# The final RMSNorm of a decoder trunk: other roots, other order, and a wider filling tile

## The chip, the cores and the metric

The kernel runs on one core of one Trainium2 chip. The metric is the device time of one execution in microseconds (us), as the median of several runs. Engines are named as in the profile: PE is TensorE (matmuls), DVE is VectorE, ACT is ScalarE, POOL is GpSimd, SP is SyncE, which here only issues DMAs. Before the change the median of three runs is 1943.36 us (1942.74 to 1943.45).

## The reference

One layer of a hybrid decoder works on 1024 tokens of width 1024 in float32. Three token mixers feed a gated merge, then comes an MLP, and a last RMSNorm over each token's row gives the output. Only the end matters here:

```python
    h = h + jnp.einsum('bsd,de->bse', merged, w_out[l])
    hn = rms_norm(h, norm_mlp_g[l])
    up = jax.nn.relu(jnp.einsum('bsd,df->bsf', hn, w_mlp_up[l]))
    h = h + jnp.einsum('bsf,fd->bsd', up * up, w_mlp_down[l])
    return rms_norm(h, final_norm_g)

def rms_norm(x, g):
    y = x * lax.rsqrt(jnp.mean(x * x, axis=-1, keepdims=True) + EPS)
    return y * g
```

So each output row is h times the gain g, times one root per row: 1/sqrt(mean of the row's squares + EPS).

## The kernel before, in words

Tokens lie in eight row blocks of 128 (0 to 7, one token per partition), and each row block of h is a tile `H[c]` of 128 by 1024, with a left half (`hsl(0)`) and a right half (`hsl(1)`) of 512 columns.

The second MLP product h + up·w_dn runs over the hidden width in four sets (`j`), each a scheme of seven bursts (`i`, 0 to 6) in place of eight plain block products. A burst is four products (`p`, 0 to 3). A product is twelve 128x512 matmuls (`seventh`, line 487: operands are split in a high and a low part, and three of the four part products are taken), and DVE then adds its result from PSUM into one half of one row block (line 1625). In the last set the order of the bursts sets which halves become final:

- burst 3: left halves of row blocks 0 to 3; burst 4: their right halves. After burst 4 these rows are finished.
- burst 5: right halves of row blocks 4 to 7; burst 6: their left halves. After burst 6 the product is at its end.

A generator (`advance(dn)`) prepares later bursts' operands between the products: ACT copies to the high part (line 132) and DVE subtracts for the low part (line 133, 128x1024), called a split below. The last three splits fall in burst 4, behind the adds of its first three products. Everything stands in a manual schedule: each engine runs its instructions in the order in which the code issues them.

The final RMSNorm, before:

- In bursts 3 to 6, behind each add, ACT squares the finished half and sums it into a column of its own (line 1843; the sum is written by a second instruction, ACTIVATION_READ_ACCUMULATOR).
- In burst 5, behind the add for row block p+4, DVE multiplies that half by the gain (line 1846), then forms the root of row block p in ten one-column instructions (`row_scale`, line 1808; `rsqrt_col`, lines 107 to 112: a bit-trick start and three Newton steps), and multiplies the whole row block p by root and gain (line 1848, 128x1024). SP stores its two halves (line 1804).
- In burst 6, POOL (for the first three) or DVE (for the last) multiplies the left half by the gain (line 1853); one product later DVE forms the root in the same ten instructions, ACT multiplies both halves by it (lines 1820 and 1816), and SP stores them. The last row block follows behind the loop; there DVE does the left half (line 1823).

A pool of small columns (`small`) holds the sums and roots; it begins with an unused tile of `SPACER` columns (line 84). Pools allocated behind it (`act`, `act1`, `act2`, `half` and others, which hold operands) lie above it, so their addresses hang on its size.

## Time and profile before

| what | value |
|---|---|
| median of three runs | 1943.36 us |
| the profiled execution's own time | 1942.18 us |
| its span, first to last instruction | 1940.5 us |
| outside the span | 1.68 us |
| PE, DVE, ACT, POOL busy | 98%, 73%, 52%, 13% |
| PE's last matmul ends | 1923.85 us after the span's start |
| from there to the end of the span | 16.65 us |

The profile has a page (busy times, chain of waits, groups of instructions) and views of the trace: the timeline lists instructions with start, duration, engine, line, operation, what is written and read, and in brackets the engine's idle time ahead of it with what ended it. The windows view gives busy times of each engine in stretches of the span. `a`, `b`, `wt`, `rt` are 128x1024 tiles of four pools, `aux` a PSUM tile, `fs` and `roots` columns. A start is in us from the start of the span.

### The profile page before, as it was taken

Reading aid. Unit: us, or ns where it says so; the run is one execution under the profiler, and the core shown is the slowest. Engines: PE = TensorE matmul, PEld = TensorE weight load, DVE = VectorE, ACT = ScalarE, POOL = GpSimd, SP = SyncE. Lnnn points to the kernel's source line nnn. Section 1 sums busy time; section 2 is a strip of 40 time slices with the busy share of each in tenths; the row PEclk is TensorE's granted clock in tenths of the full one; section 3 lists DMA queues with packets and bytes.
Section 4 is the critical chain, followed back from the end, with each engine's and each line's share of the span. In section 5 each row is a group of like instructions: output and inputs, shape, how many; then the busy total and the mean of one; then the engine's idle time right before and its main releaser. Section 6 shows DMA issues by size and latency. Waiting matters only on the chain.

```text
span 1940.5 us, 23747 instructions
## 1 busy us (share of the span) xinstructions
PE 1895.9 (98%) x8928; PEld 1581.8 (82%) x8928; DVE 1415.9 (73%) x2047; ACT 1005.3 (52%) x1463; POOL 259.0 (13%) x355
## 2 busy tenths in 40 slices
PE   8999999999999999999999999999999999999996
PEld 7998888888887787878778888887788887888885
DVE  6585868787758767677777888367666567788787
ACT  6435859676534545454554544265555555343253
POOL 4112112122342010000010110000121110000000
PEclk9999999999999999999999999999999999999998
DMA  5346575575755343434398987431553458454532
GB/s 164 77 137 141 115 157 123 122 159 136 164 137 157 110 143 110 150 106 135 113 293 276 256 233 192 152 111 49 184 201 131 168 186 282 166 163 126 178 120 87
DMA packets 211015, 301.25 MB, mean 155 GB/s; under 512 B 13028, under 2 KB 125876, under 8 KB 210900
## 3 DMA queue, kind: packets, MB, share of 16 engines
q1 hardware_dynamic: 167348, 158.54, 26.6%
q0 software_dynamic: 34544, 119.69, 23.1%
q10 hardware_dynamic: 9008, 21.51, 3.1%
q8 instruction: 70, 1.15, 0.2%
q14 instruction: 45, 0.37, 0.1%
HBM read 195.75 MB, written 74.58 MB: 139 GB/s over the span
## 4 chain that ended last, share of the span: by engine, by line
PE 81%; DVE 9%; issue 4%; ACT 3%; DMA 3%; POOL 1%; ACTq 0%; SPq 0%; POOLq 0%; DVEq 0%
PE aux L487 40%; PE ps L564 16%; PE gps L487 11%; PE aux L1387 4%; PE aux L257 4%; PE aux L800 1%; DMA raw<-in_w_in_dram 1%; PE aux L736 1%; PE aux L732 1%; DVE wt L133 1%; ACT wt L132 1%; PE aux L712 1%; PE aux L1647 1%; DVE a L133 1%; PE aux L847 0%
## 5 line engine op out<-in xcount | busy, mean ns | idle before, releaser
L564 PE MATMUL ps<-xn,wh 128*128 128x512 f32 x1088 | 295.0, 392 | 0.0
L487 PE MATMUL aux<-b,b 128*128 128x512 f32 x1152 | 264.3, 389 | 0.5 <-DVE b L133 0.5
L487 PEld LDWEIGHTS aux<-b,b 128*128 128x128 f32 x1152 | 216.0, 188 | 46.5 <-DVE b L133 1.3
L564 PEld LDWEIGHTS ps<-xn,wh 128*128 128x128 f32 x1088 | 202.9, 188 | 42.2 <-issue 0.5
L487 PE MATMUL aux<-a,b 128*128 128x512 f32 x960 | 219.4, 389 | 0.0
L487 PEld LDWEIGHTS aux<-a,b 128*128 128x128 f32 x960 | 180.2, 188 | 37.4
L564 PE MATMUL ps<-xn,wl 128*128 128x512 f32 x544 | 168.2, 389 | 0.0
L487 PE MATMUL gps<-xn,wt 128*128 128x512 f32 x684 | 158.7, 389 | 2.1 <-DVE a L238 2.1
L487 PE MATMUL aux<-b,wt 128*128 128x512 f32 x672 | 156.9, 389 | 0.0
L487 PEld LDWEIGHTS gps<-xn,wt 128*128 128x128 f32 x684 | 128.3, 188 | 29.0 <-issue 2.5
L487 PEld LDWEIGHTS aux<-b,wt 128*128 128x128 f32 x672 | 126.2, 188 | 26.2
L132 ACT ACTIVATE b<-wt 128x1024 fp32r<-128x1024 f32 x88 | 90.7, 1053 | 85.6 <-DMA wt<-u_d 63.1
L133 DVE TENSOR_TENSOR wt<-a,wt 128x1024 fp32r<-128x1024 f32 x66 | 80.8, 1225 | 65.1 <-ACT wt L132 65.0
L564 PEld LDWEIGHTS ps<-xn,wl 128*128 128x128 f32 x544 | 102.1, 188 | 21.5
L133 DVE TENSOR_TENSOR b<-wt,b 128x1024 fp32r<-128x1024 f32 x88 | 107.1, 1218 | 15.7 <-ACT b L132 15.7
L1625 DVE TENSOR_TENSOR a<-aux,a 128x512 f32<-128x512 f32 x112 | 77.0, 688 | 50.4 <-PE aux L487 50.4
L133 DVE TENSOR_TENSOR a<-a,a 128x1024 fp32r<-128x1024 f32 (+1 forms) x68 | 66.5, 985 | 41.8 <-ACT a L132 41.7
L132 ACT ACTIVATE a<-a 128x1024 fp32r<-128x1024 f32 (+1 forms) x68 | 55.7, 834 | 53.0 <-DVE a L1577 45.6
L133 DVE TENSOR_TENSOR wt<-rt,wt 128x1024 fp32r<-128x1024 f32 x35 | 42.8, 1224 | 52.7 <-ACT wt L132 52.5
L487 PE MATMUL aux<-a,wt 128*128 128x512 f32 x336 | 78.7, 390 | 1.2 <-ACT a L1500 1.2
L132 ACT ACTIVATE wt<-a 128x1024 fp32r<-128x1024 f32 x66 | 69.6, 1055 | 12.5 <-DVE a L515 12.1
L487 PEld LDWEIGHTS aux<-a,wt 128*128 128x128 f32 x336 | 62.9, 188 | 15.0 <-ACT a L1500 2.0
(348 smaller groups left out, 3505.6 us busy)
## 6 DMA issues: line engine op xcount, KB each, us to landing
wt<-u_d SPq DMA_DIRECT2D x54, 512.0 KB
u_d<-a POOLq DMA_DIRECT2D x48, 512.0 KB, 4.9
raw<-in_w_in_dram SPq DMA_DIRECT2D x34, 512.0 KB
wl<-raw POOLq DMA_DIRECT2D x34, 512.0 KB, 5.2
g_d<-a POOLq DMA_DIRECT2D x24, 512.0 KB, 3.6
a<-g_d ACTq DMA_DIRECT2D x24, 512.0 KB
rt<-in_w_in_dram SPq DMA_DIRECT2D x19, 512.0 KB
a<-in_w_in_dram SPq DMA_DIRECT2D x19, 512.0 KB
```

Of the source, the lines that this page charges most:

```text
L132: actv(dst_hi, src, AF.Copy)
L133: (eng or nc.vector).tensor_tensor(out=dst_lo, in0=src, in1=dst_hi.bitcast(F32), op=ALU.subtract)
L257: mm(ps[:, :nt], X.tok(a, k, c), wk[k][w], start=(k == 0 and i == 0), stop=(k == KD - 1 and i == 2))
L487: mm(ps, lhs[l][kk], rhs[r][kk], start=(new and n == 0), stop=(n == 11), skip_group_check=not new)
L564: mm(ps[:, hsl(h)], w[wi][:, k, :], a.rhs(ai, k, h), start=(n == 0), stop=(n == 3 * KD - 1))
L712: mm(st[:, cc * 256:cc * 256 + 256], Bt[:, 2 * q + cc, :], xw[q][:, cc].rearrange("p h d -> p (h d)"), start=True, stop=True)
L732: mm(yo[:, tok(i)], pv[c // 2][:, c % 2, j * P:(j + 1) * P], Cf[:, tok(c)], start=True, stop=True)
L736: mm(yi[64 * h:64 * h + 64, tok(i)], xdt[c // 2][:, c % 2, 2 * j + h, :], E[c // 2][:, c % 2, 2 * j + h, :], start=True, stop=True)
L800: mm(ps, w[wi][:, q * P:(q + 1) * P], S["xs"][half][ai], start=(n == 0), stop=(n == 2))
L1387: mm(ps, M.tok(a, k, c), wo[nb][k][w], start=(k == 0 and a + w == 0), stop=(k == KD - 1 and a == 1))
L1625: tt(out=h, in0=ps, in1=h, op=ALU.add)
L1647: mm(ps, w[1 + l][:, k, :], f[r][k % 4], start=(n == 0), stop=(n == 3 * KD - 1))
```

## The change

The change rewrites the final RMSNorm and leaves the products alone.

- Row blocks 0 to 3: each half is multiplied by the gain (`weigh`) already in burst 4, behind its add. The roots of all four are formed once, in burst 5 behind the first add: DVE means, ACT `Sqrt` of four columns, and DVE a reciprocal with one Newton step (`roots_first`, `refine_first`). ACT then multiplies each whole row block by its root (`rows_first`), and SP stores it in one DMA of 128x1024 in place of two.
- Row blocks 4 to 7: `weigh` on DVE for every half; POOL has no part any more. In burst 6 the right half's sum becomes a column `known`; ACT takes `Sqrt` of the scaled left sum plus `known`, and five one-column DVE instructions refine it (`refine_last`). One product later DVE multiplies the left half and ACT the right one (`out_half`). The very last store is issued by ACT's queue, all others by SP's.
- `SPACER` goes from 32 to 40 columns. With it the tiles of the pool `small` end at 52432 bytes (before: 52676), and the pools above it begin 256 bytes lower than before (`act2`, which holds the tiles `a` of this stage, at 52448 in place of 52704). The pools of the tiles `b`, `wt` and `rt` stay where they were.

```diff
-SPACER = 32
+SPACER = 40
...
+        def square_sum(c, nb):
+            actv(act()[:, :HF], H[c][:, hsl(nb)], AF.Square, accum_out=squares[c // half][nb][:, c % half:c % half + 1])
+        def weigh(c, nb):
+            if c not in scaled:
+                scaled[c] = act()
+            tt(out=scaled[c][:, hsl(nb)], in0=H[c][:, hsl(nb)], in1=fg[:, hsl(nb)], op=ALU.mult)
+        def out_half(c, nb, eng, queue):
+            o, rs = scaled[c][:, hsl(nb)], root[:, c % half:c % half + 1]
+            if eng is nc.vector:
+                ts(out=o, in0=o, scalar1=rs, scalar2=None, op0=ALU.mult)
+            else:
+                actv(o, o, AF.Identity, scale=rs)
+            queue.dma_start(out=out[c * P:(c + 1) * P, hsl(nb)], in_=o)
+        def rows_first(p):
+            o = scaled[p]
+            actv(o, o, AF.Identity, scale=root[:, p:p + 1])
+            nc.sync.dma_start(out=out[p * P:(p + 1) * P, :], in_=o)
+        def roots_first():
+            tt(out=mean, in0=squares[0][0], in1=squares[0][1], op=ALU.add)
+            ts(out=mean, in0=mean, scalar1=1.0 / D, scalar2=EPS, op0=ALU.mult, op1=ALU.add)
+            actv(root, mean, AF.Sqrt)
+        def refine_first():
+            nc.vector.reciprocal(out=root, in_=root)
+            tt(out=step_, in0=root, in1=root, op=ALU.mult)
+            tt(out=step_, in0=step_, in1=mean, op=ALU.mult)
+            ts(out=step_, in0=step_, scalar1=-0.5, scalar2=1.5, op0=ALU.mult, op1=ALU.add)
+            tt(out=root, in0=root, in1=step_, op=ALU.mult)
+        def root_last(p):
+            actv(root[:, q], squares[1][0][:, q], AF.Sqrt, scale=1.0 / D, bias=known[:, q])
+        def refine_last(p):
+            stt(out=mean[:, q], in0=squares[1][0][:, q], scalar=1.0 / D, in1=known[:, q], op0=ALU.mult, op1=ALU.add)
+            ts(out=mean[:, q], in0=mean[:, q], scalar1=-0.5, scalar2=None, op0=ALU.mult)
+            nc.vector.reciprocal(out=root[:, q], in_=root[:, q])
+            stt(out=step_[:, q], in0=root[:, q], scalar=mean[:, q], in1=root[:, q], op0=ALU.mult, op1=ALU.mult)
+            stt(out=root[:, q], in0=step_[:, q], scalar=1.5, in1=root[:, q], op0=ALU.add, op1=ALU.mult)
...
-                if i == 5:
-                    scaled[c] = act()
-                    tt(out=scaled[c][:, hsl(1)], in0=h, in1=fg[:, hsl(1)], op=ALU.mult)
-                    rs, o = row_scale(p), act()
-                    stt(out=o, in0=H[p], scalar=rs, in1=fg, op0=ALU.mult, op1=ALU.mult)
-                    for b in range(2):
-                        out_row(p, b, o[:, hsl(b)])
+                square_sum(c, nb)
+                if i == 4:
+                    weigh(c, 0)
+                    weigh(c, 1)
+                elif i == 5:
+                    if p == 0:
+                        roots_first()
+                    weigh(c, 1)
+                    if p == 0:
+                        refine_first()
+                    rows_first(p)
                 elif i == 6:
-                    eng = nc.gpsimd if p < 3 else nc.vector
-                    eng.tensor_tensor(out=scaled[c][:, hsl(0)], in0=h, in1=fg[:, hsl(0)], op=ALU.mult)
-                    if waiting is not None:
-                        last_rows(waiting, row_scale(waiting), by_scalar)
-                    waiting = c
-        last_rows(waiting, row_scale(waiting), by_vector)
+                    if p == 0:
+                        ts(out=known, in0=squares[1][1], scalar1=1.0 / D, scalar2=EPS, op0=ALU.mult, op1=ALU.add)
+                    root_last(p)
+                    weigh(c, 0)
+                    if p:
+                        out_half(c - 1, 0, nc.vector, nc.sync)
+                        out_half(c - 1, 1, nc.scalar, nc.sync)
+                    refine_last(p)
+        out_half(NCH - 1, 0, nc.vector, nc.sync)
+        out_half(NCH - 1, 1, nc.scalar, nc.scalar)
```

How the instructions stand on the engines. The first place is DVE in burst 5, the product of row block 5. Before, from the gain on (`a_15074`, behind the add of the same half) to the next add's predecessor, with the root of row block 1 between:

```order
L1846 TENSOR_TENSOR a_15074<-a_12959,a_14841 128x512
L1808 TENSOR_TENSOR fs_2290_14894<-fs_2290_14894,fs_2312_14984 128x1
L107 TENSOR_SCALAR rsq_r_15078<-fs_2290_14894 128x1
L108 TENSOR_SCALAR rsq_v_15077<-rsq_r_15078 128x1
L109 TENSOR_SCALAR rsq_r_15078<-rsq_r_15078 128x1
L111 SCALAR_TENSOR_TENSOR rsq_q_15079<-rsq_r_15078,rsq_v_15077 128x1
L112 SCALAR_TENSOR_TENSOR rsq_r_15078<-rsq_q_15079,rsq_r_15078 128x1
L111 SCALAR_TENSOR_TENSOR rsq_q_15079<-rsq_r_15078,rsq_v_15077 128x1
L112 SCALAR_TENSOR_TENSOR rsq_r_15078<-rsq_q_15079,rsq_r_15078 128x1
L111 SCALAR_TENSOR_TENSOR rsq_q_15079<-rsq_r_15078,rsq_v_15077 128x1
L112 SCALAR_TENSOR_TENSOR roots_13004<-rsq_q_15079,rsq_r_15078 128x1
L1848 SCALAR_TENSOR_TENSOR a_15089<-a_12998,roots_13004,a_14841 128x1024
```

With the change, DVE in burst 5 from the first add (row block 4) to the add of row block 6:

```order
L1625 TENSOR_TENSOR a_12957<-aux_2283_14850,a_12957 128x512
L1827 TENSOR_TENSOR fm_13008<-fs_1963_13004,fs_1964_13005 128x4
L1828 TENSOR_SCALAR fm_13008<-fm_13008 128x4
L1811 TENSOR_TENSOR a_15052<-a_12957,a_14848 128x512
L1832 RECIPROCAL fr_13009<-fr_13009 128x4
L1833 TENSOR_TENSOR fs_13010<-fr_13009 128x4
L1834 TENSOR_TENSOR fs_13010<-fs_13010,fm_13008 128x4
L1835 TENSOR_SCALAR fs_13010<-fs_13010 128x4
L1836 TENSOR_TENSOR fr_13009<-fr_13009,fs_13010 128x4
L1625 TENSOR_TENSOR a_12959<-aux_2289_14874,a_12959 128x512
L1811 TENSOR_TENSOR a_15076<-a_12959,a_14848 128x512
L1625 TENSOR_TENSOR a_12961<-aux_2297_14902,a_12961 128x512
```

A product had the add and twelve further DVE instructions; now the first has the add and eight, the other three the add and one.

The second place is DVE in burst 6, between the adds of row blocks 6 and 7. Before:

```order
L1625 TENSOR_TENSOR a_12961<-aux_2292_14897,a_12961 128x512
L1808 TENSOR_TENSOR fs_2350_15193<-fs_2350_15193,fs_2327_15071 128x1
L107 TENSOR_SCALAR rsq_r_15233<-fs_2350_15193 128x1
L108 TENSOR_SCALAR rsq_v_15232<-rsq_r_15233 128x1
L109 TENSOR_SCALAR rsq_r_15233<-rsq_r_15233 128x1
```

(six more of lines 111 and 112 follow, then the add of row block 7). With the change:

```order
L1625 TENSOR_TENSOR a_12961<-aux_2297_14902,a_12961 128x512
L1811 TENSOR_TENSOR a_15095<-a_12961,a_14848 128x512
L1816 TENSOR_SCALAR a_15076<-a_15076,fr_13009 128x512
L1844 SCALAR_TENSOR_TENSOR fm_13008<-fs_1965_13006,fk_13011 128x1
L1845 TENSOR_SCALAR fm_13008<-fm_13008 128x1
L1846 RECIPROCAL fr_13009<-fr_13009 128x1
L1847 SCALAR_TENSOR_TENSOR fs_13010<-fr_13009,fm_13008 128x1
L1848 SCALAR_TENSOR_TENSOR fr_13009<-fs_13010,fr_13009 128x1
L1625 TENSOR_TENSOR a_12963<-aux_2303_14926,a_12963 128x512
```

Ten one-column instructions became five, but two 128x512 ones came to DVE from POOL and ACT.

The third place is ACT at the first add of burst 5 (the sum of row block 4) and behind it, with the change; the table load, the `Sqrt` and the 128x1024 scaling had no counterpart on ACT there before:

```order
L1806 ACTIVATE a_15047,fs_1966_13007<-a_12957 128x512
L1829 ACT_TABLE_LOAD
L1829 ACTIVATE fr_13009<-fm_13008 128x4
L1823 ACTIVATE a_14969<-a_14969,fr_13009 128x1024
L1806 ACTIVATE a_15074,fs_1966_13007<-a_12959 128x512
```

With the change this is the only table load behind that of line 926: in burst 6 `Square`, `Sqrt` and `Identity` follow each other without one. PE's order is the same in both kernels.

More of the change, by code (lines that the diff above doesn't have):

```diff
@@ L1799, in trunk_kernel @@
                 prev.last_sum()
-        sums, scaled = {}, {}
-        roots = sm(NCH, "roots")
-        def out_row(c, nb, o):
-            nc.sync.dma_start(out=out[c * P:(c + 1) * P, hsl(nb)], in_=o)
-        def row_scale(c):
-            rs = roots[:, c:c + 1]
-            tt(out=sums[c, 0], in0=sums[c, 0], in1=sums[c, 1], op=ALU.add)
-            rsqrt_col(rs, sums[c, 0], 1.0 / D, EPS)
-            return rs
-        def last_rows(c, rs, left):
-            o = scaled[c]
-            left(o[:, hsl(0)], rs)
-            out_row(c, 0, o[:, hsl(0)])
-            actv(o[:, hsl(1)], o[:, hsl(1)], AF.Identity, scale=rs)
-            out_row(c, 1, o[:, hsl(1)])
@@ L1819, in by_scalar @@
-        def by_scalar(o, rs):
-            actv(o, o, AF.Identity, scale=rs)
-        def by_vector(o, rs):
-            ts(out=o, in0=o, scalar1=rs, scalar2=None, op0=ALU.mult)
-        waiting = None
+        half = NCH // 2
+        squares = [[sm(half, f"fs{th}{nb}") for nb in range(2)] for th in range(2)]
+        mean, root, step_, known = (sm(half, f"f{i}") for i in "mrsk")
+        scaled = {}
+        def square_sum(c, nb):
+            actv(act()[:, :HF], H[c][:, hsl(nb)], AF.Square, accum_out=squares[c // half][nb][:, c % half:c % half + 1])
@@ L1831, in trunk_kernel @@
                 nc.scalar.dma_start(out=fg, in_=final_norm_g.partition_broadcast(P))
-            for p in range(NCH // 2):
+            for p in range(half):
                 if n + p == 0:
```

5 lines of the change are left out of this document (2 added, 3 removed).

## The prediction

> **What bounds the kernel now.** I read the page first: PE sets the pace nearly everywhere, so a change behind PE's last matmul counts in full, and one beside it only if PE waits.
>
> ```profile
> span 1940.5 us, 23747 instructions
> PE 1895.9 (98%) x8928; PEld 1581.8 (82%) x8928; DVE 1415.9 (73%) x2047; ACT 1005.3 (52%) x1463; POOL 259.0 (13%) x355
> PE 81%; DVE 9%; issue 4%; ACT 3%; DMA 3%; POOL 1%; ACTq 0%; SPq 0%; POOLq 0%; DVEq 0%
> ```
>
> Next the windows view of the end, cut where DVE begins each product of burst 5 (columns: us, then PE, PEld, DVE, ACT, POOL busy, granted clock, DMA share, GB/s), and PE's last row of the timeline:
>
> ```profile
> 1902.13:1904.85 2.72, 2.72 (x13) 2.25 (x12) 0.69 (x1) 0.72 (x2) 0.00 (x0) 1.00 0.00 0
> 1909.49:1914.12 4.63, 4.63 (x22) 3.85 (x21) 4.25 (x14) 0.72 (x2) 0.00 (x0) 1.00 0.31 115
> 1923.85:1940.50 16.65, 0.00 (x1) 0.00 (x0) 11.36 (x46) 7.33 (x15) 3.76 (x3) 0.62 0.42 157
> 1912.81 11.04 PE L487 MATMUL aux<-b,b 128*128 128x512 f32 x48
> ```
>
> PE delivers a product every 2.72 us and ends at 1912.81 + 11.04 = 1923.85. DVE needs 4.63 us for each product of burst 5, so it falls 1.9 us behind each time, and 16.65 us pass after PE has ended. The timeline says what fills them:
>
> ```profile
> 1902.13 0.69 DVE L1625 TENSOR_TENSOR a<-aux,a 128x512 f32<-128x512 f32 x1 [0.90 <-PE aux L487]
> 1904.85 0.69 DVE L1625 TENSOR_TENSOR a<-aux,a 128x512 f32<-128x512 f32 x1 [2.03 <-PE aux L487]
> 1905.58 0.69 DVE L1846 TENSOR_TENSOR a<-a,a 128x512 f32<-128x512 f32 x1
> 1906.19 0.15 DVE L1808 TENSOR_TENSOR fs<-fs,fs 128x1 f32<-128x1 f32 x1
> 1924.20 2.49 POOL L1853 TENSOR_TENSOR a<-a,a 128x512 f32<-128x512 f32 x2 [296.31 <-DVE a L1625]
> 1926.08 0.63 DVE L111 SCALAR_TENSOR_TENSOR rsq_q<-rsq_r,rsq_v 128x1 f32<-128x1 f32 x1
> 1930.83 0.69 DVE L1625 TENSOR_TENSOR a<-aux,a 128x512 f32<-128x512 f32 x1
> 1934.32 0.72 ACT L1820 ACTIVATE a<-a,roots 128x512 f32<-128x512 f32 x1 [1.36 <-DVE fs L1808]
> 1936.24 0.72 ACT L1816 ACTIVATE a<-a,roots 128x512 f32<-128x512 f32 x1 [0.59 <-DVE roots L112]
> 1936.24 0.48 DVE L1823 TENSOR_SCALAR a<-a,roots 128x512 f32<-128x512 f32 x1
> ```
>
> With adds on PE's beat, the adds of row blocks 4 to 7 in burst 6 would start at 1904.85 + 4, 5, 6 and 7 times 2.72: 1915.73, 1918.45, 1921.17 and 1923.89. The last one starts at 1930.83, 6.94 us late, and then comes the root of row block 6 ahead of that of 7. The last scaling starts at 1936.24; the span ends 1940.50 - 1936.24 = 4.26 us later (the scaling, the store, its landing). So the change is priced by when the last scaling can start.
>
> **Prices.** Starts that follow each other on DVE: an add before something that needs it 0.73 us (1904.85 to 1905.58), a 128x512 multiply before something independent 0.61 (1905.58 to 1906.19). For the rest:
>
> ```profile
> 1906.56 0.15 DVE L108 TENSOR_SCALAR rsq_v<-rsq_r 128x1 f32<-128x1 f32 x1
> 1906.75 0.15 DVE L109 TENSOR_SCALAR rsq_r<-rsq_r 128x1 int32<-128x1 int32 x1
> 1906.94 0.22 DVE L111 SCALAR_TENSOR_TENSOR rsq_q<-rsq_r,rsq_v 128x1 f32<-128x1 f32 x1
> 1907.19 0.16 DVE L112 SCALAR_TENSOR_TENSOR rsq_r<-rsq_q,rsq_r 128x1 f32<-128x1 f32 x1
> 1907.39 0.22 DVE L111 SCALAR_TENSOR_TENSOR rsq_q<-rsq_r,rsq_v 128x1 f32<-128x1 f32 x1
> 60.22 0.20 DVE L222 RECIPROCAL a<-a 128x8 f32<-128x8 f32 x1
> 59.65 0.21 ACT L220 ACTIVATE a<-a 128x8 f32<-128x8 f32 x1
> 653.46 1.28 ACT L973 ACT_TABLE_LOAD   x1
> 657.28 1.06 ACT L960 ACTIVATE x<-a 128x1024 f32<-128x1024 f32 x1
> 1924.09 0.63 ACT L1843 ACTIVATE a<-a 128x512 f32<-128x512 f32 x1 [3.90 <-DVE a L1625]
> 1924.63 0.19 ACT L1843 ACTIVATION_READ_ACCUMULATOR a<-a 128x1 f32 x1
> 1924.85 0.64 DVE L1808 TENSOR_TENSOR fs<-fs,fs 128x1 f32<-128x1 f32 x1 [0.19 <-ACT a L1843]
> ```
>
> A column op with two constants costs 0.19 us, a scalar_tensor_tensor 0.25 (line 111) or 0.20 (line 112). No column reciprocal or one-column Sqrt stands in the trace; the nearest rows are 128x8, 0.20 on DVE and 0.21 on ACT. For the Sqrt with a bias column I take 0.30: a column operand adds 0.09 on ACT (0.72 with one against 0.63 without, lines 1816 and 1843). ACT's square starts about 0.79 after the add, its sum is written 0.54 later and reaches another engine 0.22 after that: 1.55 after the add.
>
> **Burst 4, added work.** Here DVE's rows before are:
>
> ```profile
> 1894.58 0.68 DVE L1625 TENSOR_TENSOR a<-aux,a 128x512 f32<-128x512 f32 x1
> 1896.69 0.69 DVE L1625 TENSOR_TENSOR a<-aux,a 128x512 f32<-128x512 f32 x1 [0.30 <-PE aux L487]
> 1900.02 1.22 DVE L133 TENSOR_TENSOR b<-wt,b 128x1024 fp32r<-128x1024 f32 x1
> ```
>
> DVE idles 0.30 to 2.03 us ahead of an add, so eight more multiplies (0.61 each) are partly hidden. Each of the first three products takes add 0.61, split 1.2, two multiplies 1.22: 3.03 us. From 1894.58 the fourth add starts at 1903.67, and with 1.95 us for it and its multiplies the first add of burst 5 at 1905.62, 0.77 late. Nobody pays: the last splits end near 1902.5, and burst 6, which needs them, starts on PE at 1912.97.
>
> **Burst 5, removed and added.** Removed from every product: ten column instructions and the 128x1024 multiply. What stays is add and multiply, 1.34 us of 2.72. The roots come once, in the first product: ACT's square from 1906.41, table load and Sqrt until about 1908.65, while DVE waits in front of the reciprocal; five column ops take 0.93, so the add of row block 5 starts at 1909.6, 2.0 late. The next starts at 1910.94 (0.65 late), the fourth on PE's beat. Queued behind DVE's wait are adds alone; PE needs row block 5's bank again at 1915.69, over 5 us later. ACT needs 0.73 + 1.06 = 1.8 us per product and stays ahead. Price on the end: nothing. Without that cushion it would be the 2.0 us.
>
> **Burst 6, the chain that remains.** Row block 4: add, `known`, multiply, then the wait for the sum until 1.55, and column ops to 2.64 us, under 2.72. Row blocks 5 and 6: add 0.73, multiply 0.61, scaling of the previous left half 0.48, column ops 0.25 + 0.19 + 0.20 + 0.25 + 0.20 = 1.09: 2.91 us, 0.19 over PE's beat each. So the last add starts at 1923.89 + 0.38 = 1924.27. The Sqrt is done 1.87 after the add (0.79 + 0.54 + 0.19 + 0.05 + 0.30), 0.4 before DVE asks for it (2.26). The last root is ready 2.91 after the add, at 1927.18, where both last scalings start; ACT's scaling of row block 6 is done by 1926.9. POOL's multiplies go away; beside them a column op took 0.63 in place of 0.22 (rows at 1924.20 and 1926.08).
>
> **The end.** For the stores: SP's issue group and the DMA view of the last 40 us in slices of 1.01 us.
>
> ```profile
> L1804 SPq DMA_DIRECT2D out_dram<-a x16: 332/332/432, 1909.6 to 1937.2; - x16
> GB/s 0 0 0 0 0 0 0 16 0 0 255 263 8 0 44 384 89 0 0 204 314 0 0 0 368 150 0 0 0 334 184 0 305 212 0 204 314 334 184 0
> 1936.00:1937.00 1.00, 0.00 (x0) 0.00 (x0) 0.65 (x3) 0.72 (x1) 0.00 (x0) 0.50 1.01 375
> ```
>
> The last four stores (256 KB each) were issued between 1935.04 (the scaling at 1934.32 done) and 1937.2; now between 1926.1 (DVE's scaling of row block 6, 1.34 + 0.48 after the last add) and 1927.9, nearly as far apart. So I keep 4.26 us behind the last scaling. The last store sits on ACT's queue, while before it was issued on SP at 1937.2, 0.24 after its scaling: 0 to 0.24 gained, of which I take none.
>
> The Trainium skill (DMA: Bandwidth & Descriptors, "Issuing engines are not separate DMA queues") says that DMAs from all issuing engines share the same 16 DMA engines and a second issuer saves only issue time; by it the forecast would at best be 0.24 us lower, where a store with a path of its own would save its 0.7 us (256 KB at 375 GB/s). The share of 1.01 at 375 GB/s agrees that the engines were full.
>
> **Sum.** 1936.24 to 1927.18 is 9.06 us. Span 1940.50 - 9.06 = 1931.4; the profiled execution 1942.18 - 9.06 = 1933.1. The median of the runs lies 1.18 above that execution, so the predicted median is 1943.36 - 9.06 = 1934.3 us. Bounds: if row blocks 5 and 6 fit into 2.72 us and the last root takes 2.64 as row block 4's, the scaling starts at 1926.53, and with 0.24 at the end the gain is 9.95: 1933.4. Upwards see the rivals.
>
> **The rivals.** (1) DVE stays late in burst 6. Every root now crosses ACT; if a product takes 3.4 us (the column ops at 0.32 each instead of 0.22), three are 2.0 late and the last root takes 3.4: scaling at 1929.3, gain 6.9, 1936.4 us. For it: a handoff per row and no slack. Against: the square's handoff is in the row at 1924.85, and POOL's disturbance goes.
>
> (2) The stores become the bound. 4.2 MB must leave, the second half from about 1920.3 (the first left half scaled, 1.34 + 0.48 after the add at 1918.45). At the 157 GB/s of the tail's row 2.1 MB take 13.4 us, until 1933.7; the last transfers ended near 1939.0 (half of the slice with 184 GB/s), 1.5 before the span's end, so the span would be 1935.2, the gain 5.3 and the median 1938.1 us. Against: that row includes waiting; slices with 368 and 384 GB/s show what a store gets.
>
> (3) Slower: the 256-byte move. Operands of most matmuls lie in pools that move; if a matmul then reads slower, PE pays everywhere. PE's 1895.9 us times 0.48% is 9.1 us: from 1.1 ns on a spacing of 2720/12 = 227 ns it eats the gain, and at 1% the kernel would end near 1943.36 + 9.9 = 1953.3 us. Against: matmuls on tiles of different pools last the same.
>
> ```profile
> L487 PE MATMUL aux<-b,b x1152: 388/389/497, 990.0 to 1923.5; 128*128 128x512 f32 x192
> L487 PE MATMUL aux<-a,wt x336: 389/389/501, 1358.8 to 1614.7; 128*128 128x512 f32 x168
> ```
>
> The `wt` and `b` pools stay and `a` moves; all have a median of 389 ns.
>
> **How the numbers follow.** Forecast 0.74, its own range 1933.0 to 1935.6; rival 1 0.12, rival 2 0.08, rival 3 0.06. The runs spread by 0.7 us; the range 1932.4 to 1937.0 holds the forecast and rival 1, about 0.8. What a measurement here can tell from no change is about 0.2%, 3.9 us. Forecast and the first two rivals lie beyond it: faster 0.93 (a point off for a mixture); rival 3 half eaten up gives 0.03 for the same, at its full size 0.04 for slower.
>
> **What would show it.** Right: PE's last matmul still near 1923.85; the last add within 0.6 us of it; POOL silent; one table load near 1907; the last scaling at 1927.2 and the span's end 4.3 later. Wrong: DVE idle in front of a reciprocal in burst 6 (rival 1), stores overlapping without a gap (rival 2), matmuls above 389 ns or a later PE end (rival 3).

## The result, and the profile after

| | before | after |
|---|---|---|
| median, six runs each | 1942.96 us (1941.71 to 1943.45) | 1932.60 us (1931.48 to 1933.57) |
| profiled execution | 1942.18 us | 1931.48 us |
| its span | 1940.5 us | 1929.8 us |
| PE's last matmul ends | 1923.85 us | 1922.49 us |
| from there to the end of the span | 16.65 us | 7.31 us |

The changed kernel takes 0.9949 of the time before (95% interval 0.9939 to 0.9959), 10.4 us less; the forecast was 1934.3 us. The page of the changed kernel has these lines to set against those of before:

```profile
span 1929.8 us, 23698 instructions
PE 1896.3 (98%) x8928; PEld 1582.3 (82%) x8928; DVE 1408.0 (73%) x2005; ACT 1010.1 (52%) x1470; POOL 254.8 (13%) x352
PE 80%; DVE 7%; issue 6%; DMA 3%; ACT 3%; POOL 1%; POOLq 0%; DVEq 0%; ACTq 0%; SPq 0%
```

They are nearly blind to what happened: PE's busy time is the same within 0.4 us, DVE's falls by 8 us of 1416, and DVE's share of the chain of waits drops from 9% to 7%. The stretch behind PE's last matmul tells more. The windows view of it (us, then PE, PEld, DVE, ACT, POOL busy, granted clock, DMA share, GB/s):

```profile
1922.49:1929.80 7.31, 0.00 (x1) 0.00 (x0) 2.94 (x9) 2.35 (x5) 0.00 (x0) 0.68 0.58 215
```

Before, this stretch held 46 instructions of DVE, three of POOL and 16.65 us; now it holds nine of DVE and none of POOL. Its 9.34 us less are the change. The other 1.36 us by which the two profiled executions differ lie ahead of it, in the time at which PE ends, and come from elsewhere (below).

The timeline of the changed kernel at the start of burst 5, with the roots of row blocks 0 to 3:

```profile
1903.82 0.69 DVE L1625 TENSOR_TENSOR a<-aux,a 128x512 f32<-128x512 f32 x1
1905.35 1.28 ACT L1829 ACT_TABLE_LOAD   x1
1906.64 0.20 ACT L1829 ACTIVATE fr<-fm 128x4 f32<-128x4 f32 x1
1906.88 0.18 DVE L1832 RECIPROCAL fr<-fr 128x4 f32<-128x4 f32 x1 [1.50 <-ACT fr L1829]
1907.77 0.68 DVE L1625 TENSOR_TENSOR a<-aux,a 128x512 f32<-128x512 f32 x1
1909.10 0.68 DVE L1625 TENSOR_TENSOR a<-aux,a 128x512 f32<-128x512 f32 x1
1911.65 0.69 DVE L1625 TENSOR_TENSOR a<-aux,a 128x512 f32<-128x512 f32 x1 [1.15 <-PE aux L487]
```

DVE stands still for 1.50 us in front of the reciprocal while ACT loads its table, and the add of row block 5 comes late for it. The add of row block 7 already waits for PE again: the delay is gone three products later. The same view for burst 6 and the end:

```profile
1911.45 11.04 PE L487 MATMUL aux<-b,b 128*128 128x512 f32 x48
...
1914.37 0.69 DVE L1625 TENSOR_TENSOR a<-aux,a 128x512 f32<-128x512 f32 x1 [1.30 <-PE aux L487]
1917.09 0.69 DVE L1625 TENSOR_TENSOR a<-aux,a 128x512 f32<-128x512 f32 x1 [0.29 <-PE aux L487]
1919.81 0.69 DVE L1625 TENSOR_TENSOR a<-aux,a 128x512 f32<-128x512 f32 x1
1922.53 0.69 DVE L1625 TENSOR_TENSOR a<-aux,a 128x512 f32<-128x512 f32 x1
1923.26 0.69 DVE L1811 TENSOR_TENSOR a<-a,a 128x512 f32<-128x512 f32 x1
1923.87 0.48 DVE L1816 TENSOR_SCALAR a<-a,fr 128x512 f32<-128x512 f32 x1
1924.01 0.29 ACT L1840 ACTIVATE fr<-fs,fk 128x1 f32<-128x1 f32 x1
1924.26 0.15 DVE L1844 SCALAR_TENSOR_TENSOR fm<-fs,fk 128x1 f32<-128x1 f32 x1
1924.45 0.15 DVE L1845 TENSOR_SCALAR fm<-fm 128x1 f32<-128x1 f32 x1
1924.52 0.15 DVE L1846 RECIPROCAL fr<-fr 128x1 f32<-128x1 f32 x1
1924.71 0.22 DVE L1847 SCALAR_TENSOR_TENSOR fs<-fr,fm 128x1 f32<-128x1 f32 x1
1924.96 0.16 DVE L1848 SCALAR_TENSOR_TENSOR fr<-fs,fr 128x1 f32<-128x1 f32 x1
1925.15 0.72 ACT L1818 ACTIVATE a<-a,fr 128x512 f32<-128x512 f32 x1 [0.24 <-DVE fr L1848]
1925.91 0.34 ACTq L1819 DMA_DIRECT2D out_dram<-a  x1
```

The adds follow each other every 2.72 us, PE's own beat, and the last one starts 1922.53 - 1922.49 = 0.04 us after PE has ended (before: 6.98). The last scaling starts 2.62 us after the last add.

### The profile page after: what moved, and what is told of

Same layout as the page of the kernel before. It is cut to its first block, busy times and chain, and to the rows that moved or that the text cites. A ratio compares the mean times of both kernels' runs of the same rounds, so it can differ in the third digit from the quotient of the medians.

```text
span 1929.8 us, 23698 instructions
## 1 busy us (share of the span) xinstructions
PE 1896.3 (98%) x8928; PEld 1582.3 (82%) x8928; DVE 1408.0 (73%) x2005; ACT 1010.1 (52%) x1470; POOL 254.8 (13%) x352
## 4 chain that ended last, share of the span: by engine, by line
PE 80%; DVE 7%; issue 6%; DMA 3%; ACT 3%; POOL 1%; POOLq 0%; DVEq 0%; ACTq 0%; SPq 0%
PE aux L487 40%; PE ps L564 16%; PE gps L487 10%; PE aux L1387 5%; PE aux L257 4%; PE aux L800 1%; DMA c<-yc_d 1%; PE aux L736 1%; DMA raw<-in_w_in_dram 1%; PE aux L732 1%; DVE wt L133 1%; PE aux L712 1%; DVE a L133 1%; ACT wt L132 1%; DMA a<-g_d 1%
## 5 line engine op out<-in xcount | busy, mean ns | idle before, releaser
L133 DVE TENSOR_TENSOR wt<-rt,wt 128x1024 fp32r<-128x1024 f32 x35 | 42.8, 1224 | 52.6 <-ACT wt L132 52.5
```

What stands on the lines that cost most here:

```text
L133: (eng or nc.vector).tensor_tensor(out=dst_lo, in0=src, in1=dst_hi.bitcast(F32), op=ALU.subtract)
```

## Experiments on the roots

Unless said otherwise a kernel is the changed one with the edit shown, and the median before that stands beside it was taken on the same chip at the same time. Medians repeat within about 1 us, so the mechanism is read from positions in the trace that are counted from PE's last matmul:

| kernel | last add starts | last scaling starts | span ends | median us | ratio to before (95%) |
|---|---|---|---|---|---|
| before | +6.98 | +12.39 | +16.65 | 1942.96 | 1 |
| old roots | +5.87 | +9.69 | +14.20 | 1939.94 | 0.9988 (0.9979 to 0.9997) |
| no weighing ahead | +1.16 | +3.78 | +8.44 | 1934.28 | 0.9957 (0.9942 to 0.9971) |
| gain on POOL | +0.38 | +3.00 | +7.61 | 1933.74 | 0.9954 (0.9939 to 0.9969) |
| after | +0.04 | +2.66 | +7.31 | 1932.60 | 0.9949 (0.9939 to 0.9959) |
| scaling early | +0.04 | +2.67 | +7.12 | 1933.01 | 0.9948 (0.9932 to 0.9965) |
| scaling early, no Newton step | +0.04 | +2.05 | +6.58 | 1933.08 | 0.9951 (0.9936 to 0.9965) |

**The changed kernel once more**, nothing edited:

> The changed kernel once more, as the measure for the others. In its first profile PE's last matmul ended at 1922.49 us, 1.36 us earlier than before the change, though PE's order is the same. Theory (start-up scatter): this moves from execution to execution by about 1 us either way and belongs to the first 100 us and the stage around 600 us, so PE's end lies anywhere from 1921.5 to 1925 here, while the stretch behind it repeats: last scaling 2.66 us and end of span 7.3 us (within 0.1) after PE's end. Rival (the 256-byte move speeds PE up): PE's end lies at 1922.5 within 0.3 again, always about 1.4 below the kernel before. Median 1932 to 1934 us.

1933.61 us against 1942.22 (ratio 0.9953, 0.9941 to 0.9966). PE ends at 1924.74 here, 2.25 us later than in the first profile, and the last scaling follows 2.66 us and the end 7.26 us behind it. The end of the kernel repeats; the time at which PE gets there doesn't.

**Old roots.** Weighing ahead, ACT's scaling and everything else stay, but each row block gets its root in ten column instructions on DVE again:

```diff
+        def old_root(sums, p):
+            tt(out=mean[:, p:p + 1], in0=sums[0][:, p:p + 1], in1=sums[1][:, p:p + 1], op=ALU.add)
+            rsqrt_col(root[:, p:p + 1], mean[:, p:p + 1], 1.0 / D, EPS)
...
                 elif i == 5:
-                    if p == 0:
-                        roots_first()
                     weigh(c, 1)
-                    if p == 0:
-                        refine_first()
+                    old_root(squares[0], p)
                     rows_first(p)
                 elif i == 6:
...
-                    root_last(p)
                     weigh(c, 0)
...
-                    refine_last(p)
+                    old_root(squares[1], p)
```

> Weighing ahead without the new roots: burst 4 multiplies by the gain as in the change, ScalarE scales row blocks 0 to 3 whole, but every root is formed by VectorE's old ten column instructions, row by row. Theory (the column instructions carry the delay): a product of burst 5 costs VectorE 0.73 + 0.61 + 2.1 = 3.4 us against PE's 2.72, one of burst 6 3.8, so the last add comes about 6 us after PE's beat and the last scaling about 10 us after PE's end (before 12.4, changed 2.7): most of the gain is lost, median 1939 to 1941. Rival (the 128x1024 multiply taken off VectorE carries the gain): last scaling within 5 us of PE's end, median below 1936.

1939.94 us against 1942.22: of the gain some 2 us are left. Its timeline, the last three adds and the last scaling:

```profile
1922.76 0.69 DVE L1625 TENSOR_TENSOR a<-aux,a 128x512 f32<-128x512 f32 x1
1926.47 0.68 DVE L1625 TENSOR_TENSOR a<-aux,a 128x512 f32<-128x512 f32 x1
1930.17 0.69 DVE L1625 TENSOR_TENSOR a<-aux,a 128x512 f32<-128x512 f32 x1
1933.99 0.72 ACT L1818 ACTIVATE a<-a,fr 128x512 f32<-128x512 f32 x1 [1.76 <-DVE fr L112]
```

A product of burst 6 costs DVE 3.71 us here (one of burst 5 3.30), against PE's 2.72, and no add of the two bursts is preceded by a wait for PE: DVE is the bound of bursts 5 and 6, as in the kernel before. The last scaling starts 9.69 us behind PE's end. So, with everything else of the change in place, the shorter roots are worth 9.69 - 2.66 = 7.0 us of the 12.39 - 2.66 = 9.7 us gained there.

**No weighing ahead.** The roots are new, but row blocks 0 to 3 are multiplied by root and gain in one DVE instruction in burst 5, as before the change:

```diff
         def rows_first(p):
-            o = scaled[p]
-            actv(o, o, AF.Identity, scale=root[:, p:p + 1])
+            o = act()
+            stt(out=o, in0=H[p], scalar=root[:, p:p + 1], in1=fg, op0=ALU.mult, op1=ALU.mult)
...
-                if i == 4:
-                    weigh(c, 0)
-                    weigh(c, 1)
-                elif i == 5:
+                if i == 5:
```

> The new roots without weighing ahead: burst 4 has no multiplies by the gain, and VectorE multiplies row blocks 0 to 3 by root and gain in one 128x1024 instruction each in burst 5, as before. Theory (the column instructions carried the delay): a product of burst 5 costs 0.73 + 0.61 + 1.2 = 2.54 us, under PE's 2.72, so the delay of about 2 us from the one root is worked off slowly and the last add is 0 to 0.6 us late; last scaling 2.7 to 3.3 us after PE's end, median within 1 us of the changed kernel. Rival (weighing ahead matters by itself): last scaling 5 us or more after PE's end, median 1935 or more.

1934.28 us against 1943.38. The timeline of its burst 5 (line 1823 is that instruction) and its last add:

```profile
1909.42 1.29 DVE L1823 SCALAR_TENSOR_TENSOR a<-a,fr,a 128x1024 f32<-128x1024 f32 x1
1910.62 0.68 DVE L1625 TENSOR_TENSOR a<-aux,a 128x512 f32<-128x512 f32 x1
1911.95 1.28 DVE L1823 SCALAR_TENSOR_TENSOR a<-a,fr,a 128x1024 f32<-128x1024 f32 x1
1913.15 0.68 DVE L1625 TENSOR_TENSOR a<-aux,a 128x512 f32<-128x512 f32 x1
...
1925.52 0.68 DVE L1625 TENSOR_TENSOR a<-aux,a 128x512 f32<-128x512 f32 x1
```

A product of burst 5 takes DVE 2.53 us, 0.19 less than PE's beat, so the delay at its start is worked off too slowly: the last add comes 1.16 us behind PE's end, the last scaling 3.78 instead of 2.66. I had put it at 2.7 to 3.3. Weighing ahead in burst 4 is worth 1.1 us on the path, and in the medians it can't be told from nothing.

**Gain on POOL.** The left halves of row blocks 4 to 6 are multiplied by the gain on POOL, as before the change:

```diff
-                    weigh(c, 0)
+                    weigh(c, 0, nc.gpsimd.tensor_tensor if p < 3 else tt)
```

> The changed kernel with the left halves of row blocks 4 to 6 multiplied by the gain on GpSimd again, as before the change (1.25 us each there, 0.61 on VectorE). Theory: VectorE's column instructions beside GpSimd take up to 0.6 us again, but a product of burst 6 has 0.6 us less work and 0.3 us to spare, so last scaling 2.6 to 3.3 us after PE's end; median within 1 us of the changed kernel. Rival (taking GpSimd out of the tail is what made it short): column instructions at 0.6 us push the last scaling to 4 us or more after PE's end.

1933.74 us against 1943.38; the last scaling 3.00 us behind PE's end. Its timeline, row block 6 and the add behind it:

```profile
1921.26 1.47 POOL L1811 TENSOR_TENSOR a<-a,a 128x512 f32<-128x512 f32 x1 [1.40 <-DVE a L1625]
1921.97 0.77 DVE L1844 SCALAR_TENSOR_TENSOR fm<-fs,fk 128x1 f32<-128x1 f32 x1 [0.40 <-ACT a L1806]
1923.37 0.68 DVE L1625 TENSOR_TENSOR a<-aux,a 128x512 f32<-128x512 f32 x1
```

The column instruction of line 1844, 0.15 us in the changed kernel, lasts 0.77 and ends at 1922.74, when POOL's multiply ends (1921.26 + 1.47 = 1922.73). The product becomes 2.87 us long (1920.50 to 1923.37) and costs 0.15 over PE's beat. The Trainium skill (SBUF — State Buffer, "Who interferes with whom") says that a DVE instruction with two SBUF inputs contends with a GpSimd instruction that reads SBUF, that the ports they share are an exclusive lock, and that the order of issue decides who blocks. The trace agrees: in all three products with a POOL multiply the instruction of line 1844 started later and ended with POOL's to 0.01 or 0.02 us. Taking the gain from POOL to DVE costs DVE 0.61 us per product, of which 0.40 fill the wait in the bracket, and saves it the 0.62 by which line 1844's instruction was held up.

**Scaling early.** ACT multiplies the right half of row blocks 4 to 6 right behind its own root and not one product later:

```diff
                     if p:
                         out_half(c - 1, 0, nc.vector, nc.sync)
-                        out_half(c - 1, 1, nc.scalar, nc.sync)
                     refine_last(p)
+                    if p < 3:
+                        out_half(c, 1, nc.scalar, nc.sync)
```

> ScalarE scales the right half of row blocks 4 to 6 right behind its own root, not one product later, so these stores leave about 1.8 us earlier. It asks why the end of the span comes 4.65 us after the last scaling with the change and 4.26 us before it. Theory (the last four stores, 1 MB in about 1.5 us of issue, wait for each other at 375 GB/s): with one of them out of the way the end comes 4.0 to 4.3 us after the last scaling. Rival (the store on ScalarE's queue lands later): it stays at 4.65. The last scaling stays 2.6 to 2.7 us after PE's end.

1933.01 us against 1943.38. The span ends 4.45 us behind the last scaling (1928.85 to 1933.3), against 4.65 in the changed kernel. It lies between what the two theories expected: queueing of the last stores explains 0.2 us of the 4.65 at most, not the 0.4 by which it exceeds the 4.26 of before. What else it is, the account of the prediction shows.

**Scaling early, no Newton step.** This kernel also leaves out the Newton step of row blocks 4 to 7, so that their roots are the plain reciprocal of ACT's square root:

```diff
-            stt(out=mean[:, q], in0=squares[1][0][:, q], scalar=1.0 / D, in1=known[:, q], op0=ALU.mult, op1=ALU.add)
-            ts(out=mean[:, q], in0=mean[:, q], scalar1=-0.5, scalar2=None, op0=ALU.mult)
             nc.vector.reciprocal(out=root[:, q], in_=root[:, q])
-            stt(out=step_[:, q], in0=root[:, q], scalar=mean[:, q], in1=root[:, q], op0=ALU.mult, op1=ALU.mult)
-            stt(out=root[:, q], in0=step_[:, q], scalar=1.5, in1=root[:, q], op0=ALU.add, op1=ALU.mult)
```

> As the one before, and the roots of row blocks 4 to 7 without the Newton step: ScalarE's Sqrt and VectorE's reciprocal alone, so these roots are as exact as the Sqrt is. Theory: behind the last add the chain is sum 1.5, Sqrt 0.3, reciprocal 0.2: last scaling 2.0 to 2.1 us after the add in place of 2.62, and the end of the span 6.2 to 6.5 us after PE's end (7.3 with the change). Rival (VectorE's multiply and scaling ahead of the root set the last scaling): 2.4 us or more after the add.

1933.08 us against 1943.38. The end of its timeline:

```profile
1924.36 0.69 DVE L1625 TENSOR_TENSOR a<-aux,a 128x512 f32<-128x512 f32 x1 [0.75 <-PE aux L487]
1926.17 0.16 DVE L1844 RECIPROCAL fr<-fr 128x1 f32<-128x1 f32 x1
1926.37 0.72 ACT L1818 ACTIVATE a<-a,fr 128x512 f32<-128x512 f32 x1 [0.23 <-DVE fr L1844]
```

The chain behind the last add shrinks from 2.62 to 2.01 us, as expected, and DVE gets 0.75 us of slack per product. The end is 6.58 us behind PE's (6.2 to 6.5 had been expected), 0.7 less than in the changed kernel and the shortest of all. The median doesn't show it, and the reason is the next point.

**Where PE's end comes from.** PE's last matmul ends between 1922.49 and 1926.18 in nine executions of eight kernels, those of the table above and the one with a filler of 104 columns below, which all run the same matmuls with their operands laid out alike. Two groups of PE's instructions (duration in ns min/median/max, then first and last start), the transposes of line 448 and the matmuls of line 1387, show where that arises. In the changed kernel:

```profile
L448 PE MATMUL aux<-ident,wT x8: 272/273/273, 68.3 to 69.1; 128*128 128x128 f32 x8
L1387 PE MATMUL aux<-a,b x240: 387/389/482, 1223.9 to 1299.8; 128*128 128x512 f32 x120
```

And in its second run:

```profile
L448 PE MATMUL aux<-ident,wT x8: 271/273/273, 69.8 to 70.6; 128*128 128x128 f32 x8
L1387 PE MATMUL aux<-a,b x240: 387/389/482, 1226.2 to 1302.1; 128*128 128x512 f32 x120
```

From the first of these matmuls of line 1387 to PE's end it is 1922.49 - 1223.9 = 698.6 us in the one and 1924.74 - 1226.2 = 698.5 us in the other. All of the difference of 2.25 us is there before: 1.5 us by the first transposes, at 68.3 and 69.8, the rest between them and line 1387. An execution brings a scatter of up to 3.7 us (1922.49 to 1926.18) with it from its first part, and beside that a difference of 0.7 us at the end can't be seen in a median of four.

## Experiments on the filling tile

The prediction held the addresses to be a small risk (rival 3), from which the wider filler (`SPACER`) might lose something. These runs turn the question round: what does the filler save?

**The changed kernel without it.**

```diff
-SPACER = 40
+SPACER = 32
```

> The changed kernel with the filling tile at its old 32 columns: the pools behind it now lie 288 bytes lower than before the change, no longer a multiple of 64 bytes. Theory (addresses do not matter): median within 1.5 us of the changed kernel run beside it, matmul durations still 389 ns, the stretch behind PE's end 7.3 us. Rival (operand addresses matter modulo 64 to 256 bytes): PE's matmuls on tiles of the moved pools, or VectorE's or ScalarE's instructions on them, last longer; 0.5% on PE would be +9 us.

1947.86 us against 1942.22, a ratio of 1.0029 (1.0018 to 1.0041): the change without its filler is slower than the kernel before, and the theory that addresses do not matter fell. The end is as good as ever (last scaling 2.65 us behind PE's last matmul), but PE ends at 1938.58. The groups of line 487, the matmuls of the products:

```profile
L487 PE MATMUL aux<-b,b x1152: 387/389/504, 992.2 to 1938.2; 128*128 128x512 f32 x192
L487 PE MATMUL aux<-a,b x960: 395/396/397, 1158.0 to 1927.3; 128*128 128x512 f32 x192
L487 PE MATMUL aux<-a,wt x336: 392/396/498, 1364.9 to 1623.6; 128*128 128x512 f32 x168
L487 PE MATMUL aux<-h,wt x228: 392/395/632, 603.8 to 968.6; 128*128 128x512 f32 x114
```

The changed kernel has a median of 389 ns in all four. In a matmul the first operand named streams through and the second is loaded as weights. Those with both from pool `b` keep their 389 ns; those that read one from a pool that moved and one from a pool that stayed take 396, and of the 960 `a,b` none takes under 395. The 960, the 336 and the 240 of line 1387 times 7 ns make 10.8 us; from the first of those 240 to PE's end this kernel takes 1938.58 - 1229.7 = 708.9 us, 10.3 more than the changed one. Some five more come ahead of line 1387, most of them from 456 matmuls on the half tiles `h` (medians of 395 and 396 ns, 389 in the changed kernel), from 144 on pairs `c,b` (mean 396 against 389) and from the first 96 of the 960.

**A filler of 104 columns** puts the pools at exactly the addresses of the kernel before, 256 bytes above those of the change:

```diff
-SPACER = 40
+SPACER = 104
```

> The changed kernel with 104 filling columns: the operand pools lie at exactly the addresses of the kernel before. Theory (addresses do not matter): median within 1.5 us of the changed kernel, PE's end anywhere from 1921.5 to 1925. Rival (the 256-byte move gave the 1.36 us by which PE ended earlier): PE's end back at 1923.8 and the median 1.4 us above the changed kernel in every execution.

1932.66 us against 1942.22 (0.9952, 0.9938 to 0.9965). Nothing moves: the 256 bytes cost and bring nothing, and the filler matters only for what it keeps.

**The kernel before with a wider filler**, for the other direction:

```diff
-SPACER = 32
+SPACER = 40
```

> The kernel before with nothing but the filling tile at 40 columns: its left-hand pools move up by 32 bytes. In the run with 32 columns in the changed kernel, matmuls with one operand in a moved pool and the other in an unmoved one took 396 ns against 389, and PE's end came 15.5 us later. There the pools started at a multiple of 64 bytes, the unmoved ones 32 above a multiple. Theory (the two operands of a matmul must start alike modulo 64): here the same mismatch, so PE's end comes 14 to 17 us later and the median is 1956 to 1959 us, with the end of the program untouched. Rival (only the distance of 288 bytes, or the new final part, brings it): the median stays at 1943.

1957.87 us against 1943.01, a ratio of 1.0077 (1.0062 to 1.0092), as expected. So it isn't the new code that suffers from the addresses: the old code does too. The filler's size hangs on the other columns in its pool. With 32 columns of filler the new, fewer columns bring the pools down by 288 bytes (from 52704 to 52416); the eight columns more, 32 bytes, make it 256.

**Which alignment counts.** Three more kernels vary the starts of the pools. The filler of 56 columns moves the left pools by 64 bytes against the changed kernel:

```diff
-SPACER = 40
+SPACER = 56
```

> The changed kernel with 56 filling columns: the moved pools start alike with the others modulo 64 bytes, but not modulo 128 (32 against 96). Theory (modulo 64 is what counts): matmuls at 389 ns, median within 1.5 us of the changed kernel's 1932 to 1934. Rival (modulo 128 or 256 counts): 396 ns again for mixed operands, median near 1948.

Two kernels have unused tiles ahead of the pools, here with 8 columns (32 bytes) on both sides:

```diff
     base = ctx.enter_context(tc.tile_pool(name="base", bufs=1))
+    padl = ctx.enter_context(tc.tile_pool(name="padl", bufs=1))
+    padl.tile([P, 8], F32, tag="pad", name="padl")
     wp = ctx.enter_context(tc.tile_pool(name="w", bufs=6))
...
     normed = ExitStack()
+    padp = ctx.enter_context(tc.tile_pool(name="padr", bufs=1, side="right"))
+    padp.tile([P, 8], F32, tag="pad", name="padr")
```

> The changed kernel with 32 bytes of padding put ahead of the other pools, on the left and on the right, so that all operand pools start at a multiple of 64 bytes. Theory (only the operands' being alike counts): 389 ns, median 1932 to 1934. Rival (a start 32 above a multiple of 64 is the good one): matmuls above 389 ns for every pair and a median above 1948. Other rival (a multiple of 64 is better): below 389 ns and a median under 1930.

and here with 24 columns (96 bytes) on the left and 8 on the right:

```diff
+    padl = ctx.enter_context(tc.tile_pool(name="padl", bufs=1)).tile([P, 24], F32, tag="pad", name="padl")
...
+    padr = ctx.enter_context(tc.tile_pool(name="padr", bufs=1, side="right")).tile([P, 8], F32, tag="pad", name="padr")
```

> The changed kernel with 96 bytes of padding on the left and 32 on the right: all operand pools start 64 bytes above a multiple of 128 (before and with the change: 96 above), the left ones 64 and the right ones 192 above a multiple of 256. Before this the kernel with the pools alike modulo 64 but not 128 lost 8 us, and the one with the left pools at 0 and the right ones at 64 modulo 128 lost 21. Theory (a matmul's two operands must start alike modulo 128 bytes, and where they start does not matter): 389 ns for all pairs, median 1932 to 1934 us. Rival (they must be alike modulo 256): pairs of a left and a right pool above 389 ns, median above 1938. Other rival (96 above a multiple of 128 is the good start): all pairs above 389 ns, also those of two tiles of one pool.

Both theories behind these runs fell. That it is enough to be alike modulo 64 bytes fell with the 56 columns, at 1941.18 us; that 128 is enough, with the last kernel, at 1958.85, the slowest of all. The kernel with 32 bytes on both sides has all its pools at multiples of 64 bytes, as its expectation said, but not alike in more than that: in these programs the pools on the right are laid from the far end downwards, so the pad moved them the other way (down by 32, to 163776), and they lay 64 bytes off the left ones. With the addresses of the tiles in each program the kernels sort themselves. Start of the streamed operand minus start of the weights, modulo 256 bytes, with the median of line 487's matmuls in ns:

| kernel | `a,b` | `a,wt` | `b,wt` | `b,b` | first transpose to PE's end, us | median us |
|---|---|---|---|---|---|---|
| before | 0: 389 | 0: 389 | 0: 389 | 0: 389 | 1855.3 | 1942.96 |
| after | 0: 389 | 0: 389 | 0: 389 | 0: 389 | 1854.2 | 1932.60 |
| filler of 104 | 0: 389 | 0: 389 | 0: 389 | 0: 389 | 1854.7 | 1932.66 |
| filler of 56 | 64: 392 | 64: 392 | 0: 389 | 0: 389 | 1862.5 | 1941.18 |
| before, filler of 40 | 32: 396 | 32: 396 | 0: 389 | 0: 389 | 1870.2 | 1957.87 |
| filler of 32 | 224: 396 | 224: 396 | 0: 389 | 0: 389 | 1870.1 | 1947.86 |
| 32 bytes on both sides | 64: 392 | 0: 389 | 192: 394 | 0: 389 | 1875.5 | 1953.98 |
| 96 and 32 bytes | 128: 394 | 0: 389 | 128: 395 | 0: 389 | 1881.2 | 1958.85 |

The rows of the last kernel, for one:

```profile
L487 PE MATMUL aux<-b,b x1152: 388/389/504, 1001.9 to 1949.1; 128*128 128x512 f32 x192
L487 PE MATMUL aux<-a,b x960: 387/394/398, 1167.6 to 1938.2; 128*128 128x512 f32 x192
L487 PE MATMUL aux<-b,wt x672: 387/395/398, 1360.3 to 1628.3; 128*128 128x512 f32 x168
L487 PE MATMUL aux<-a,wt x336: 389/389/498, 1375.3 to 1634.6; 128*128 128x512 f32 x168
```

And those of the kernel with 32 bytes on both sides (line 491 is line 487 of the others):

```profile
L491 PE MATMUL aux<-b,wt x672: 394/394/397, 1359.1 to 1627.4; 128*128 128x512 f32 x168
L491 PE MATMUL aux<-a,wt x336: 387/389/505, 1374.1 to 1633.6; 128*128 128x512 f32 x168
```

In both, `a` and `wt` moved together, and their matmuls stay at 389 ns although both start elsewhere than in the changed kernel; what counts is the one start against the other. `b,wt`, which no filler touches, becomes dear as soon as the two sides part. In the table a difference of 0 modulo 256 costs nothing, 64 some 3 ns, and 32, 128, 192 and 224 some 5 to 7. Other differences weren't tried. Why the addresses act in this way isn't settled by these runs.

## Why the prediction was right

The mechanism held step by step. The sum of its terms came within 0.3 us of what was measured behind PE's end because two errors, 0.67 us of gain not counted and 0.39 us of cost not counted, partly cancelled, and that part is luck.

- **PE's end** was to stay at 1923.85. It came to 1922.49 in the profiled execution and to 1924.74 in another one of the same kernel. The difference to before is the scatter of the beginning, which the prediction didn't have; the runs around 1923.85 lie within it. It can also explain why the median fell by 10.4 us and the stretch behind PE's end by 9.34: in the second run of the same kernel the median lay 8.6 us below that of before (1942.22 to 1933.61). So the 1.7 us between the forecast median and the measured one tell little about the mechanism.
- **Burst 4 and 5.** The first add of burst 5 was put at 0.77 us late, the second at 2.0, the third at 0.65, with nobody paying. Against the add at 1911.65, which is on PE's beat, they were 0.33, 1.56 and 0.17 late, and nobody paid. (In the last product of burst 4 the add takes 0.60 us and not 0.73, since the multiply behind it needs the other half.) The cushion is real, and it is what the run without weighing ahead lacks: there DVE gains 0.19 us per product on PE in place of 1.39 (2.72 less the 1.33 from 1907.77 to 1909.10).
- **Row blocks 5 and 6**, the term "2.91 us, 0.19 over PE's beat each", was sized too high. From the add at 1922.53 the rows give 0.73 for it, 0.61 for the multiply, 0.39 for the scaling (I had taken its 0.48 of duration as the distance to the next start) and 0.89 for the column instructions to the root (I had 1.09): 2.62. The reciprocal starts 0.07 us behind the instruction ahead of it, with which it has nothing to do (I had 0.19 there), and the `scalar_tensor_tensor` of line 1844, whose scalar is a constant, costs 0.19 like those of line 112; the 0.25 that I took for it is the price of those whose scalar is a column (lines 111 and 1847). An add that needs nothing of a root follows its last instruction after 0.07, so a product could be 2.50 us short, and it was just that in burst 6 without weighing ahead (1923.02 to 1925.52). The last add was on the beat, 0.38 us earlier than forecast, and the chain behind it 0.29 shorter. That is nearly the lower bound that the prediction gave.
- **The end behind the last scaling**, "unchanged at 4.26", came out at 4.65. The windows view of the changed kernel shows where the last data left:

```profile
1927.00:1928.00 1.00, 0.00 (x0) 0.00 (x0) 0.00 (x0) 0.00 (x0) 0.00 (x0) 0.50 0.99 369
1928.00:1929.00 1.00, 0.00 (x0) 0.00 (x0) 0.00 (x0) 0.00 (x0) 0.00 (x0) 0.50 0.01 2
```

The transfers end at about 1928.0, the span 1.8 us later. Before they ended at about 1939.0, 1.5 us ahead of the end. These 0.3 us aren't the stores, nor the queue of ACT. In the single packets and semaphore events that the trace records, the last store has landed 0.34 to 0.35 us behind its last packet in every run, on either queue (at 1939.44 before, at 1928.44 with the change). Behind it SP works through the waits for the eight semaphores of its program's DMAs one after the other, and these are what is left of them when it has landed, its own among them, before (from 1939.2 us on) and with the change (from 1928.2 on):

```profile
L1882 SPq EVENT_SEMAPHORE x3: 28/28/28, 1939.5 to 1939.6; - x3
L1911 SPq EVENT_SEMAPHORE x8: 27/28/28, 1928.5 to 1928.9; - x8
```

They start 0.06 us apart. Before, the last store belonged to the sixth semaphore of the list; with the change it belongs to the first, so the other seven are waited for behind it although they are long done: five waits more, 0.30 us. From the last landing to the end it is 1.03 us with three waits left (before), 1.27 with seven (old roots, scaling early with and without the Newton step) and 1.33 with eight (after). The other 0.1 us of the 0.39 lies in the stores: from the start of the last scaling to the last packet it is 2.86 us before and 2.94 with the change.

The 0.24 us that I had named as a possible gain of ACT's queue didn't come. By the Trainium skill (DMA: Bandwidth & Descriptors, "Issuing engines are not separate DMA queues") a second issuer saves only the time of issuing. The trace agrees: the last store was issued 0.04 us behind its scaling (1925.91), but its first packet ran at 1927.25, when SP's last store was nearly through, and the stores ran one behind the other at 369 GB/s.
- **The sum.** 9.06 us forecast; 0.38 and 0.29 more gained, 0.39 more paid: 9.34 measured, behind PE's end.
- **Rivals 1 and 2** didn't come. In burst 6 the trace lists no wait of DVE for ACT's square root (the reciprocal at 1924.52 has no idle time ahead of it), and a column instruction takes 0.18 us on average, not 0.32. The last stores do follow each other without a gap (a DMA share of 0.99), but the kernel with the early scaling puts that at 0.2 us at most, not at the 3.8 by which rival 2 lay above the forecast.
- **Rival 3** was given little, 0.06, for a poor reason. "Matmuls on tiles of different pools last the same" was true of the rows, but in the kernel before all pools happen to start alike modulo 256 bytes, so these rows couldn't show what a difference costs. As far as that argument goes it was luck that nothing was lost. The one that would have carried is the number 256: the change moves the pools by just the step that costs nothing. Had the filler stayed at 32, the same prediction would have been off by 13 to 14 us and wrong in sign.

## What to carry to other kernels

Price work behind the last matmul by the queue of its engine: here ten column instructions at 0.2 us each made DVE fall 0.6 to 1 us behind PE with each product (the run with the old roots), and 1.9 us together with the 128x1024 multiply, and only the sum at the very end was to be seen. Take them away first, and place what is left where DVE idles anyway. When a change adds or removes any tile, look at the starts of the operands of all matmuls modulo 256 bytes ahead of looking at the change itself: a pool that lies 32 bytes off made over 1,500 matmuls 7 ns longer each, which is more than the 9.34 us that this change gains at the end.

## What the runs showed of the hardware that was not expected

- A float32 matmul of 128 by 512 whose two SBUF operands start at different addresses modulo 256 bytes takes 392 to 396 ns in place of 389 (medians, at the five differences tried: 32, 64, 128, 192 and 224 bytes). In this kernel that made 7 to 27 us from the first transpose to PE's end.
- The first part of an execution scatters by up to 3.7 us, in part ahead of the first transposes at 68 to 70 us; from 1224 us to PE's end the nine executions with operands alike agree within 0.1 us (698.5 to 698.6).
- The last store's landing came 0.34 to 0.35 us behind its last packet, whether ACT's queue or SP's had issued it. From there to the end of the span it was 1.03, 1.27 or 1.33 us, by how many of SP's closing waits (three, seven or eight, 0.06 us each) were left then, that for the store itself among them.
